# Seven groups of RWKV matmuls per head pair tied to fixed places in the projection's stream of set matmuls

## The chip, the cores and the metric

The kernel runs on one core of one Trainium2 chip. The metric is the device time of one launch, in microseconds. A core has a tensor engine (TensorE, PE in the profile), a vector engine (VectorE, DVE), a scalar engine (ScalarE, ACT), GpSimd (POOL) and a queue engine that starts transfers (SyncE, SP). Each engine works through its own list of instructions, whose order is settled when the kernel is built; between engines, semaphores hold an instruction back until what it needs is done.

## The reference

One block of a hybrid decoder, for 512 tokens of width 2048, all in float32. The projection `h @ w_in` feeds three things: an RWKV-7 mixer with 16 heads of 64, a sliding-window attention, and two sigmoid gates of 2048 columns each. The change concerns the mixer and the stretch in which it runs beside the projection.

```python
z = h @ w_in[l]
zs = token_shift(z[..., :RW_SHIFT_COLS], rw_mu[l])
o_rw = rwkv7_mix(zs, ...)            # 16 heads, 512 steps each
...
def step(state, inp):                # inside rwkv7_mix
    r_t, k_t, v_t, w_t, ka_t, kb_t = inp
    sa = einsum('bhvk,bhk->bhv', state, ka_t)
    state = state * w_t[:, :, None, :] + sa[..., None] * kb_t[:, :, None, :] + v_t[..., None] * k_t[:, :, None, :]
    y = einsum('bhvk,bhk->bhv', state, r_t)
    return state, y
...
y = group_norm(y) * gn_w + gn_b
out = (y + bonus) * g
...
x = x + (sigmoid(zg_rw) * (o_rw @ w_rw) + sigmoid(zg_att) * (o_att @ w_att)) @ w_out
x = x + conv_ffn(rms_norm(x, norm2_g[l]), w_up, conv_w, conv_b, w_down)
```

## The kernel before, in words

The program has three long parts: the projection with attention and the RWKV mixer beside it, the two output matrices, and the feed-forward network. All products of float32 are kept exact enough by splitting each operand into a high and a low part and adding three products (high by high, low by high, high by low).

**The stream of set matmuls.** `project` makes one projection tile of 128 columns by 512 tokens: 16 slices of the width, three matmuls each, 48 in all, into one PSUM tile `acc` (lines 263 to 265). Their weights come from `load_w`: a transfer into `raw` (L245), a copy to the high part `whi` on ScalarE (L248), a subtraction to the low part `wlo` on VectorE (L249); one load holds four slices, that is 12 set matmuls. I call these matmuls the stream, or set matmuls. They depend on nothing that the mixer does.

**The pairs.** The 16 heads are worked on two at a time, in eight pairs (0 to 7). The 512 tokens are cut into eight chunks of 64. For pair p, `late(p)` solves the recurrence; `early(p+1)` prepares the next pair, with its three projection tiles (k, r, v); `final(p)` normalises and gates the result; then three gate tiles are projected. So beside each pair run six tiles, 288 set matmuls. The steps of `late` and `final`, in order:

1. Masked products of each chunk (L634): 16 matmuls into four PSUM tiles from a rotation of three buffers named `bulk`; VectorE masks each (L638, L639).
2. The inverse of a triangular matrix per chunk. Its first level: transposes of BX (L651), VectorE and ScalarE work on them (L653, L655, splits at L212 and L213); transposes of BKK (L668) that ScalarE copies out (L669).
3. Transposes of `vz` (L672, the first group that the change names), which ScalarE copies to UV and SV (L678).
4. Five levels m = 2, 4, 8, 16, 32 that double the block solved: `mm3` with AI (L684, L685), the sum of two halves (ScalarE L697, VectorE L698), a mask (L708), a split into XIW (ScalarE L212, VectorE L213), then `mm3` with BT (the same lines; these are the second to sixth groups that the change names), its sum, and transposes of X (L730) whose copies give the next level's BT (L734).
5. A serial chain over the eight chunks: psG (L742), copied to GY (L743), psU (L745), copied to UV (L746 and L747), psS (L751), which updates the state SV (L755) for the next chunk.
6. Group norm of y on VectorE and ScalarE (L769 to L776), its last operation the product at L776.
7. `final`: transposes of y (L783, the seventh group), copied on ScalarE (L789), scaled and added on VectorE (L790, L791), six matmuls for the gate (L795), a product (L796) and a transfer out on POOL (L797).

**What sets the order.** The framework's scheduler lists every instruction and lays each engine's order out from the dependences and its own estimates of time, except where the code asks for program order. The mixer's groups are thereby strewn among set matmuls on TensorE, and the weight splits L248 and L249 among the mixer's work on ScalarE and VectorE. Whether a group waits on the chip depends on how many set matmuls stand ahead of it.

Of the kernel before, what the change touches and what calls it, by code (L numbers as in the profile page):

```python
# [18 lines left out]
P = 128  # L19
# [115 lines left out]
def block_kernel(ctx: ExitStack, tc: tile.TileContext, d: Dims, a: dict, out: bass.AP):  # L135
    nc = tc.nc
    act, dve, pool, pe, sync = nc.scalar, nc.vector, nc.gpsimd, nc.tensor, nc.sync
    NK, NP, NQ, NKV, NF = d.NK, d.NP, d.NQ, d.NKV, d.NF
# [19 lines left out]
    ident = const.tile([P, P], F32, name="ident")  # L158
# [61 lines left out]
    for f in range(NPRE):  # L220
        w, t = a["w_up"][f], {n: up_d[f, n] for n in ("s3", "s1", "P6", "P3")}
# [12 lines left out]
    def sums_along(jobs=jobs):  # L234
# [3 lines left out]
        pin(sync.dma_start(dst, first, max_dma_last_dim=4096))  # L238
        return lambda: pool.dma_start(dst, second, accum_op=ALU.add, max_dma_last_dim=4096)

    def load_w(src):
        nk, ncol = src.shape[1:]
        n = nk * ncol
        raw = wp["raw"].tile([P, 512], F32, name="raw", tag="raw")[:, :n].rearrange("p (k c) -> p k c", c=ncol)
        wp["last"] = sync.dma_start(raw, src)  # L245
        hi = wp["hl"].tile([P, 512], F32R, name="whi", tag="whi")[:, :n].rearrange("p (k c) -> p k c", c=ncol)
        lo = wp["hl"].tile([P, 512], F32R, name="wlo", tag="wlo")[:, :n].rearrange("p (k c) -> p k c", c=ncol)
        act.activation(hi, raw, AF.Copy)  # L248
        dve.tensor_tensor(lo, raw, hi.bitcast(F32), op=ALU.subtract)  # L249
        wp["n"] += 1  # L250
        if wp["n"] % wp["step"] == 0:
            sums_along()()
        return hi, lo

    def project(acc, src, xhi, xlo, pre=()):
        nk = src.shape[1]
        for k0 in range(0, nk, 4):
            n = min(4, nk - k0)
            whi, wlo = pre[k0 // 4] if k0 // 4 < len(pre) else load_w(src[:, k0 : k0 + n])
            for j in range(n):  # L260
                k = k0 + j
                first, last = k == 0, k == nk - 1
                pe.matmul(acc, whi[:, j], xhi[:, k], start=first, stop=False)  # L263
                pe.matmul(acc, whi[:, j], xlo[:, k], start=False, stop=False)  # L264
                pe.matmul(acc, wlo[:, j], xhi[:, k], start=False, stop=last)  # L265


    act.dma_start(par, a["par"])
# [17 lines left out]
    if True:  # L286
        xhi = by_k(big(big1, "xhi", "h1"))
        xlo = by_k(big(big1, "xlo", "l1"))
        zt = {c: a["w_z"][i].rearrange("p (k c) -> p k c", c=P) for i, c in enumerate(d.z_tiles())}
        with tc.tile_pool(name="x0_ps", bufs=6, space=PSUM) as ps0:  # L290
# [9 lines left out]
            first = {d.c_ka: [load_w(zt[d.c_ka][:, k0 : k0 + 4]) for k0 in range(0, min(NK, 12), 4)]}  # L300
# [22 lines left out]
        def emit_gate():  # L323
            if not gates:
                return
            i = gates.pop(0)
            acc = ztile(d.c_zr + i * P)
            g = gp.tile([P, S], F32, name="gt", tag="gt")
            act.activation(g, acc, AF.Tanh, scale=0.5)
            act.dma_start(gate_d[i * P : (i + 1) * P], g)  # L330
# [19 lines left out]
        with ExitStack() as pt:  # L350
# [32 lines left out]
            for t in range(NKV):  # L383
                acc = ztile(d.c_ka + t * P)
# [90 lines left out]
        with ExitStack() as pr:  # L475
# [131 lines left out]
            def late(p, st):  # L607
# [61 lines left out]
                    act.activation(W2[:, ns, 0:4:3], ps.rearrange("p n (h c) -> p n h c", c=C), AF.Copy)  # L669
                ps = bulk().rearrange("p (t c) -> p t c", c=P)  # L670
                for t in range(NT):
                    pe.transpose(ps[:, t], vz[:, t * P : (t + 1) * P], ident)  # L672
                for dst in (UV, SV):
                    dst = dst.rearrange("p (t w) h c -> p t w h c", w=2)
                    for w, (rl, rh) in enumerate(HV):
# [5 lines left out]

                def mm3(ps, wt, both, hi):
                    for n in range(NCH):
                        pe.matmul(ps[:, n], wt[:, 0, n], both(n), start=True, stop=False)  # L684
                        pe.matmul(ps[:, n, 0], wt[:, 1, n], hi(n), start=False, stop=True)  # L685

                def halves(m, t):
# [91 lines left out]
            def final(p, st):  # L779
                ag, bon, y = st  # L780
                ps = bulk().rearrange("p (t c) -> p t c", c=P)
                for t in range(NT):
                    pe.transpose(ps[:, t], y[:, t * P : (t + 1) * P], ident)  # L783
                yc = wtile("gn")
                dst = yc.rearrange("p (t w c) -> p t w c", w=2, c=C)
                for w, (rl, rh) in enumerate(HV):
                    for h, (lo, hi) in enumerate(HV):
                        ol, oh = HV[1 - h]
                        act.activation(dst[lo:hi, :, w], ps[rl:rh, :, ol:oh], AF.Copy)  # L789
                dve.tensor_scalar(yc, yc, col("gn_w", p), col("gn_b", p), op0=ALU.mult, op1=ALU.add)  # L790
                dve.tensor_tensor(yc, yc, bon, op=ALU.add)  # L791
                ps = bulk()
                for i in range(NG):
                    for j, (l, r) in enumerate(((0, 0), (0, 1), (1, 0))):
                        pe.matmul(ps, ag[l][:, i], gdz[r][:, i], start=i + j == 0, stop=i == NG - 1 and j == 2)  # L795
                dve.tensor_tensor(yc, yc, ps, op=ALU.mult)  # L796
                pool.dma_start(o_rw_d[p], yc)  # L797

            st = early(0)
            for p in range(NP):  # L800
                lt = late(p, st)
                if p + 1 < NP:
                    st = early(p + 1)
                final(p, lt)
                sums_along(up_jobs)()
                for _ in range(GATES_PER_PAIR * NK // 16):
                    emit_gate()


        xbs = ExitStack()  # L810
# [653 lines left out]
```

## Time and profile before

| what | value |
|---|---|
| median of three runs | 2811.76 us (2809.82 to 2811.87) |
| profiled execution, its own time | 2812.58 us |
| its span | 2810.7 us |
| TensorE busy | 2764.8 us (98%) |
| VectorE, ScalarE, POOL busy | 71%, 48%, 8% |
| start of pairs 0 to 7 (first L634) | 332.74, 431.79, 529.27, 626.90, 724.69, 822.33, 919.97, 1017.56 us |

The eight pairs fill the span from about 333 to 1115 us; all else lies outside the change. In a line of the profile's timeline stand start, duration, engine, line, operation, tiles, shapes, and in brackets how long the engine stood idle before and who released it. The two starts in the table for one pair may differ by 0.1 to 0.2 us from those of a row, where a row begins with a weight load.

### The profile page before, as it was taken

To read this page: it belongs to the slowest core of one execution; us is meant where nothing else is said; L and a number is where in the kernel's file an instruction comes from. 1 tells how busy PE (TensorE), PEld (TensorE's weight loads), DVE (VectorE), ACT (ScalarE), POOL (GpSimd) and SP (SyncE) were. 2 spreads that over 40 slices of the span, in tenths; PEclk is the share of its full clock that TensorE was granted. 3 is DMA by queue.
4 is the path that set the end of the run, shared out by engine and by line. 5 is a ranking of instruction groups with operands and counts; after the bars stand their busy time and mean duration, and the time that the engine had idled before them with its cause. 6 is when DMAs were issued, how large, how long until landed. Compare 5 with 4: busy or idle time off the path is not lost.

```text
span 2810.7 us, 45990 instructions
## 1 busy us (share of the span) xinstructions
PE 2764.8 (98%) x17466; PEld 2403.0 (85%) x17466; DVE 1990.5 (71%) x3452; ACT 1352.5 (48%) x2278; POOL 232.1 (8%) x307
## 2 busy tenths in 40 slices
PE   7999999999999999999999999999999999999999
PEld 5777777787777777888889999999999999888887
DVE  4588677777787775455678787777777778655555
ACT  4255445445544543322466555554555455444444
POOL 0001010110101001011000010101010101000000
PEclk9999999999999999999999999999999999999999
DMA  7855787777778777888785888988888888877775
GB/s 220 228 157 156 207 207 180 194 199 182 189 179 204 177 176 193 263 244 288 248 266 178 227 227 232 245 229 221 236 244 227 222 239 231 321 241 242 257 255 188
DMA packets 227182, 619.62 MB, mean 220 GB/s; under 512 B 24832, under 2 KB 44944, under 8 KB 225936
## 3 DMA queue, kind: packets, MB, share of 16 engines
q1 hardware_dynamic: 158400, 441.03, 48.5%
q0 software_dynamic: 37216, 136.33, 25.3%
q10 hardware_dynamic: 31344, 39.31, 4.0%
q8 instruction: 137, 2.24, 0.3%
q14 instruction: 85, 0.70, 0.1%
HBM read 566.96 MB, written 191.18 MB: 270 GB/s over the span
## 4 chain that ended last, share of the span: by engine, by line
PE 88%; DVE 6%; ACT 3%; issue 1%; DMA 1%; SPq 0%; ACTq 0%; DVEq 0%
PE X L1104 18%; PE X L968 11%; PE acc L264 9%; PE acc L263 9%; PE acc L265 9%; PE Y L1104 9%; PE Y L968 9%; PE Z L1104 4%; DVE wlo L249 1%; PE psS L751 1%; PE bulk L634 1%; PE psG L742 1%; PE bulk L684 1%; ACT whi L248 1%; PE mi L463 1%
## 5 line engine op out<-in xcount | busy, mean ns | idle before, releaser
L263 PE MATMUL acc<-xhi,whi 128*128 128x512 f32 x1152 | 463.4, 402 | 1.9 <-DVE xlo L309 1.9
L265 PE MATMUL acc<-xhi,wlo 128*128 128x512 f32 x1152 | 461.2, 400 | 0.0
L264 PE MATMUL acc<-xlo,whi 128*128 128x512 f32 x1152 | 460.6, 400 | 0.0
L248 ACT ACTIVATE whi<-raw 128x512 fp32r<-128x512 f32 x352 | 220.2, 630 | 376.0 <-PE acc L264 298.2
L961 DVE TENSOR_TENSOR wlo<-raw,whi 128x1024 fp32r<-128x1024 f32 x210 | 257.1, 1225 | 199.7 <-ACT whi L960 199.7
L249 DVE TENSOR_TENSOR wlo<-raw,whi 128x512 fp32r<-128x512 f32 x352 | 241.7, 689 | 169.4 <-ACT whi L248 155.0
L960 ACT ACTIVATE whi<-raw 128x1024 fp32r<-128x1024 f32 x210 | 222.7, 1061 | 283.8 <-PE X L968 137.0
L1087 DVE TENSOR_TENSOR wlo<-raw,whi 128x1024 fp32r<-128x1024 f32 x184 | 224.8, 1223 | 77.5 <-ACT whi L1085 77.2
L1104 PE MATMUL X<-b,whi 128*128 128x256 f32 x1472 | 268.9, 283 | 0.2 <-ACT whi L1085 0.2
L1104 PE MATMUL X<-t,whi 128*128 128x256 f32 x1408 | 257.2, 283 | 1.4 <-ACT u L1132 1.4
L1104 PE MATMUL Y<-t,whi 128*128 128x256 f32 x1408 | 257.1, 283 | 0.0
L263 PEld LDWEIGHTS acc<-xhi,whi 128*128 128x128 f32 x1152 | 217.5, 189 | 41.5 <-DVE xlo L309 2.1
L264 PEld LDWEIGHTS acc<-xlo,whi 128*128 128x128 f32 x1152 | 217.6, 189 | 39.8 <-issue 1.7
L265 PEld LDWEIGHTS acc<-xhi,wlo 128*128 128x128 f32 x1152 | 217.3, 189 | 39.8 <-issue 0.9
L1104 PEld LDWEIGHTS X<-b,whi 128*128 128x128 f32 x1472 | 229.6, 192 | 0.5 <-ACT whi L1085 0.4
L1085 ACT ACTIVATE whi<-a 128x1024 fp32r<-128x1024 f32 x124 | 130.9, 1056 | 201.6 <-DVE a L1080 193.7
L1104 PEld LDWEIGHTS X<-t,whi 128*128 128x128 f32 x1408 | 219.6, 192 | 1.6 <-ACT u L1132 1.6
L1104 PEld LDWEIGHTS Y<-t,whi 128*128 128x128 f32 x1408 | 219.6, 192 | 0.0
L1104 PE MATMUL X<-b,wlo 128*128 128x256 f32 x736 | 208.5, 283 | 0.9 <-DVE wlo L1087 0.9
L1085 ACT ACTIVATE whi<-raw 128x1024 fp32r<-128x1024 f32 x184 | 192.9, 1049 | 22.8 <-ACT whi L1085 14.1
L1087 DVE TENSOR_TENSOR wlo<-a,whi 128x1024 fp32r<-128x1024 f32 x124 | 152.0, 1226 | 67.5 <-ACT whi L1085 66.9
L1104 PE MATMUL X<-t,wlo 128*128 128x256 f32 x704 | 199.5, 283 | 0.2 <-DVE wlo L1087 0.2
(387 smaller groups left out, 5801.7 us busy)
## 6 DMA issues: line engine op xcount, KB each, us to landing
raw<-in_w_up_dram SPq DMA_DIRECT2D x170, 512.0 KB
raw<-in_w_z_dram SPq DMA_DIRECT2D x288, 256.0 KB
s_dn<-in_w_dn_dram POOLq DMA_DIRECT2D x88, 512.0 KB, 6.6
raw<-s_dn SPq DMA_DIRECT2D x88, 512.0 KB
raw<-in_w_up_dram POOLq DMA_DIRECT2D x80, 512.0 KB, 8.5
raw<-in_w_dn_dram SPq DMA_DIRECT2D x66, 512.0 KB
s_dn<-in_w_dn_dram SPq DMA_DIRECT2D x44, 512.0 KB
s_dn<-s_dn SPq DMA_DIRECT2D x44, 512.0 KB
```

What stands on the lines that cost most here:

```text
L248: act.activation(hi, raw, AF.Copy)
L249: dve.tensor_tensor(lo, raw, hi.bitcast(F32), op=ALU.subtract)
L263: pe.matmul(acc, whi[:, j], xhi[:, k], start=first, stop=False)
L264: pe.matmul(acc, whi[:, j], xlo[:, k], start=False, stop=False)
L265: pe.matmul(acc, wlo[:, j], xhi[:, k], start=False, stop=last)
L463: pe.matmul(ps, vhl[:, n - 1 + kb, g].rearrange("p e c -> p (e c)"), phl[i][:, kb].rearrange("p h c -> p (h c)"), start=kb == kbs[0] and i ...
L960: act.activation(whi, wr, AF.Copy)
L961: dve.tensor_tensor(wlo, wr, whi.bitcast(F32), op=ALU.subtract)
L968: pe.matmul(dst, l[:, q, ts], r[:, es], start=fst and j == 0, stop=lst and j == 2, skip_group_check=True)
L1085: pin(act.activation(hi, t, AF.Copy))
L1087: return lambda: pin(dve.tensor_tensor(lo, t, hi.bitcast(F32), op=ALU.subtract))
L1104: pin(pe.matmul(ps, l[:, k], r[:, k], start=start and k + i == 0, stop=last and i == 2, skip_group_check=True))
```

## The change

A list `stream` takes every set matmul in program order. Of each pair a list `entries` takes seven instructions: the first transpose of vz, the first BT matmul of each of the five levels, and the first transpose of y. For pairs 1 to 6, each entry gets an ordering dependence (no semaphore, only a rule for the scheduler) behind the set matmul that is the 23rd, 46th, 75th, 102nd, 127th, 154th or 282nd since the pair began. Pairs 0 and 7 get none.

```diff
+    stream = []
+
+    def behind(ins, before):
+        tc.add_manual_dep(ins.ins, before.ins.name,
+                          mybir.DependencyInfo(mybir.DependencyClass.NoSync, mybir.DependencyReason.DATA))
+
...
-                pe.matmul(acc, whi[:, j], xhi[:, k], start=first, stop=False)
-                pe.matmul(acc, whi[:, j], xlo[:, k], start=False, stop=False)
-                pe.matmul(acc, wlo[:, j], xhi[:, k], start=False, stop=last)
+                stream.append(pe.matmul(acc, whi[:, j], xhi[:, k], start=first, stop=False))
+                stream.append(pe.matmul(acc, whi[:, j], xlo[:, k], start=False, stop=False))
+                stream.append(pe.matmul(acc, wlo[:, j], xhi[:, k], start=False, stop=last))
...
-                    pe.transpose(ps[:, t], vz[:, t * P : (t + 1) * P], ident)
+                    ins = pe.transpose(ps[:, t], vz[:, t * P : (t + 1) * P], ident)
+                    if t == 0:
+                        entries.append(ins)
...
-                        pe.matmul(ps[:, n], wt[:, 0, n], both(n), start=True, stop=False)
+                        ins = pe.matmul(ps[:, n], wt[:, 0, n], both(n), start=True, stop=False)
+                        if wt is BT and n == 0:
+                            entries.append(ins)
...
-                    pe.transpose(ps[:, t], y[:, t * P : (t + 1) * P], ident)
+                    ins = pe.transpose(ps[:, t], y[:, t * P : (t + 1) * P], ident)
+                    if t == 0:
+                        entries.append(ins)
...
+            entries = []
+            ZT = 3 * NK
+            LATER = (23, 46, ZT + 27, 2 * ZT + 6, 2 * ZT + 31, 3 * ZT + 10, 5 * ZT + 42)
             st = early(0)
             for p in range(NP):
+                entries.clear()
+                base = len(stream)
                 lt = late(p, st)
...
+                if 0 < p < NP - 1:
+                    for ins, at in zip(entries, LATER):
+                        behind(ins, stream[base + at - 1])
```

ZT is 48, the set matmuls of a tile. Every engine executes the same instructions as before; only their order differs, from pair 1 on. In set matmuls since the pair's first L634, pairs 2 to 6 (pair 1 in brackets where it differs):

| group | before | after |
|---|---|---|
| vz transposes | 21 | 23 |
| BT of level 2 | 46 | 47 (46) |
| BT of level 4 | 73 | 75 |
| BT of level 8 | 98 | 102 |
| BT of level 16 | 121 | 127 |
| BT of level 32 | 146 | 154 |
| first psG, last psS | 146, 230 | 154, 238 |
| y transposes | 264 | 282 |
| next pair's L634 | 288 | 288 |

In the new code the lines stand 6 to 12 further down: the set matmuls at 269 to 271, the splits at 254 (ScalarE) and 255 (VectorE), L634 as 640, L638 and L639 as 644 and 645, `mm3` as 692 and 695, L783 as 793, L795 as 807, L796 as 808.

On TensorE, at the end of pair 2, around the transposes of y (the numbers tell one buffer from the next; `whi_6480` is a weight load, after which `whi_6500` and `whi_6518` are the last two that the pair's stream uses):

```order
L264 MATMUL acc_6459<-xlo_203,whi_6480 128x512
L265 MATMUL acc_6459<-xhi_202,wlo_6481 128x512
L783 MATMUL bulk_6278<-ident_162,yc_5836 128x128 x4
L795 MATMUL bulk_6290<-gdhi_2606,wghi_4875 128x512
L795 MATMUL bulk_6290<-gdlo_2607,wghi_4875 128x512
L795 MATMUL bulk_6290<-gdhi_2606,wglo_4876 128x512
```

Before, y stood at the end of load 6480's twelve set matmuls, with the 24 of the two last loads still behind it. After the change:

```order
L270 MATMUL acc_6459<-xlo_203,whi_6518 128x512
L271 MATMUL acc_6459<-xhi_202,wlo_6519 128x512
L793 MATMUL bulk_6278<-ident_162,yc_5836 128x128 x4
L807 MATMUL bulk_6290<-gdhi_2606,wghi_4875 128x512
L807 MATMUL bulk_6290<-gdlo_2607,wghi_4875 128x512
L807 MATMUL bulk_6290<-gdhi_2606,wglo_4876 128x512
```

Now y stands in the middle of the last load, 6518: eighteen set matmuls moved from behind y to ahead of it, and six are left between the gate's matmuls and the next pair's L634.

Also on TensorE, at level 4 of pair 2 (XIW by BT into a `bulk` tile); the weights with the number 6144 and 6145 are one load, whose first set matmul stood directly ahead of the group:

```order
L264 MATMUL acc_6105<-xlo_203,whi_6126 128x512
L265 MATMUL acc_6105<-xhi_202,wlo_6127 128x512
L263 MATMUL acc_6105<-xhi_202,whi_6144 128x512
L684 LDWEIGHTS BT_2939
L684 MATMUL bulk_5632<-XIW_5457,BT_2939 128x64
L685 LDWEIGHTS BT_2939
```

After the change:

```order
L270 MATMUL acc_6105<-xlo_203,whi_6126 128x512
L271 MATMUL acc_6105<-xhi_202,wlo_6127 128x512
L269 MATMUL acc_6105<-xhi_202,whi_6144 128x512
L270 MATMUL acc_6105<-xlo_203,whi_6144 128x512
L271 MATMUL acc_6105<-xhi_202,wlo_6145 128x512
L692 LDWEIGHTS BT_2939
L692 MATMUL bulk_5632<-XIW_5457,BT_2939 128x64
```

The group now has the two further set matmuls L270 and L271 ahead of it.

On VectorE, at the boundary from pair 2 to pair 3, from the split after y's last product to the first masks of the next pair:

```order
L249 TENSOR_TENSOR wlo_7085<-raw_7082,whi_7084 128x512
L790 TENSOR_SCALAR gn_6283<-gn_6283,par_164 128x512
L213 TENSOR_TENSOR wglo_7056<-wl_7053,wghi_7055 128x256
L791 TENSOR_TENSOR gn_6283<-gn_6283,bon_5186 128x512
L796 TENSOR_TENSOR gn_6283<-gn_6283,bulk_6290 128x512
L249 TENSOR_TENSOR wlo_7103<-raw_7100,whi_7102 128x512
L249 TENSOR_TENSOR wlo_7121<-raw_7118,whi_7120 128x512
L638 TENSOR_TENSOR AB_2940<-bulk_6549,cst_168 128x256
L639 TENSOR_TENSOR W2_2937<-bulk_6549,cst_168 128x2x128
L638 TENSOR_TENSOR AB_2940<-bulk_6554,cst_168 128x256
L639 TENSOR_TENSOR W2_2937<-bulk_6554,cst_168 128x2x128
L646 TENSOR_TENSOR tt_6548<-AB_2940,cst_168 64x256
```

After the change:

```order
L786 TENSOR_TENSOR yc_5836<-yc_5836,rg1_5947 128x512
L255 TENSOR_TENSOR wlo_7103<-raw_7100,whi_7102 128x512
L802 TENSOR_SCALAR gn_6283<-gn_6283,par_164 128x512
L213 TENSOR_TENSOR wglo_7056<-wl_7053,wghi_7055 128x256
L803 TENSOR_TENSOR gn_6283<-gn_6283,bon_5186 128x512
L808 TENSOR_TENSOR gn_6283<-gn_6283,bulk_6290 128x512
L255 TENSOR_TENSOR wlo_7121<-raw_7118,whi_7120 128x512
L644 TENSOR_TENSOR AB_2940<-bulk_6549,cst_168 128x256
L645 TENSOR_TENSOR W2_2937<-bulk_6549,cst_168 128x2x128
L644 TENSOR_TENSOR AB_2940<-bulk_6554,cst_168 128x256
L645 TENSOR_TENSOR W2_2937<-bulk_6554,cst_168 128x2x128
L644 TENSOR_TENSOR AB_2940<-bulk_6559,cst_168 128x256
```

Of the two weight splits that stood between the gate's product and the first mask (L638, now L644) one is left, and the product L646 has gone from among the masks to behind them.

## The prediction

> **What bounds the kernel now.** I read the page first: busy time of each engine, the chain that ended last, the costliest groups.
>
> ```profile
> PE 2764.8 (98%) x17466; PEld 2403.0 (85%) x17466; DVE 1990.5 (71%) x3452; ACT 1352.5 (48%) x2278; POOL 232.1 (8%) x307
> ...
> PE 88%; DVE 6%; ACT 3%; issue 1%; DMA 1%; SPq 0%; ACTq 0%; DVEq 0%
> ...
> L263 PE MATMUL acc<-xhi,whi 128*128 128x512 f32 x1152 | 463.4, 402 | 1.9 <-DVE xlo L309 1.9
> ...
> L248 ACT ACTIVATE whi<-raw 128x512 fp32r<-128x512 f32 x352 | 220.2, 630 | 376.0 <-PE acc L264 298.2
> ...
> L249 DVE TENSOR_TENSOR wlo<-raw,whi 128x512 fp32r<-128x512 f32 x352 | 241.7, 689 | 169.4 <-ACT whi L248 155.0
> ```
>
> TensorE is the bound, so a new order can win only what TensorE stands still, and the set matmuls of this line hardly wait themselves (1.9 us in 1152). The two splits of their weights, 0.63 us on ScalarE and 0.69 on VectorE, serve below. The table by stage shows the pairs that the change touches; each stretch runs from one pair's first L634 to the next.
>
> ```profile
> core 0: us, PE busy (x) PEld busy (x) DVE busy (x) ACT busy (x) POOL busy (x), PEclk, DMA share, GB/s
> ...
> 431.79:529.27 97.48, 96.06 (x636) 77.06 (x635) 75.25 (x182) 47.78 (x107) 9.87 (x13) 1.00 0.75 190
> 529.27:626.90 97.63, 96.22 (x637) 77.21 (x635) 75.37 (x182) 47.93 (x107) 9.85 (x13) 1.00 0.75 189
> ```
>
> A pair lasts 97.63 us at full clock with 1.4 us of idle TensorE; no engine beside it is near its limit. The waits of six pairs name whom TensorE waits for:
>
> ```profile
> PE bulk L684 <- DVE XIW L213: 4.3, 12, 0.6
> PE bulk L783 <- DVE yc L776: 2.7, 6, 0.5
> ```
>
> That is two waits a pair at L684 and one at L783, two of the kinds of groups that the change ties down. The busy end of a matmul is modelled, so I price each wait by starts instead. Here is the timeline of TensorE in pair 2: the set matmul ahead of each of the seven groups, and the group's first instruction; and one group (L751) that didn't wait.
>
> ```profile
> 539.11 0.47 PE L265 MATMUL acc<-xhi,wlo 128*128 128x512 f32 x1
> 539.60 0.66 PE L672 MATMUL bulk<-ident,vz 128*128 128x128 f32 x4
> ...
> 546.34 0.39 PE L263 MATMUL acc<-xhi,whi 128*128 128x512 f32 x1
> 547.27 0.20 PE L684 MATMUL bulk<-XIW,BT 128*128 128x64 f16 x1 [0.54 <-DVE XIW L213]
> ...
> 554.80 0.39 PE L263 MATMUL acc<-xhi,whi 128*128 128x512 f32 x1
> 555.35 0.20 PE L684 MATMUL bulk<-XIW,BT 128*128 128x64 f16 x1 [0.16 <-DVE XIW L213]
> ...
> 562.36 0.39 PE L264 MATMUL acc<-xlo,whi 128*128 128x512 f32 x1
> 562.86 0.20 PE L684 MATMUL bulk<-XIW,BT 128*128 128x64 f16 x1
> ...
> 569.39 0.39 PE L263 MATMUL acc<-xhi,whi 128*128 128x512 f32 x1
> 569.72 0.20 PE L684 MATMUL bulk<-XIW,BT 128*128 128x64 f16 x1
> ...
> 576.73 0.39 PE L264 MATMUL acc<-xlo,whi 128*128 128x512 f32 x1
> 577.23 0.20 PE L684 MATMUL bulk<-XIW,BT 128*128 128x64 f16 x1
> ...
> 610.35 0.40 PE L264 MATMUL acc<-xlo,whi 128*128 128x512 f32 x1
> 610.67 0.66 PE L751 MATMUL psS<-UV,W 128*128 128x64 f32 x4
> 611.14 0.48 PE L265 MATMUL acc<-xhi,wlo 128*128 128x512 f32 x1
> ...
> 618.73 0.39 PE L265 MATMUL acc<-xhi,wlo 128*128 128x512 f32 x1
> 619.57 0.66 PE L783 MATMUL bulk<-ident,yc 128*128 128x128 f32 x4 [0.45 <-DVE yc L776]
> ...
> 621.46 0.39 PE L263 MATMUL acc<-xhi,whi 128*128 128x512 f32 x1
> ...
> 626.90 3.61 PE L634 MATMUL bulk<-BAR,BKK 128*128 128x256 f32 x16
> ```
>
> Between the last two rows lie 24 set matmuls in 5.44 us: one each 0.227 us. The gaps less 0.23 are the waits: 0.70 us at level 2 (BT2), then 0.32, 0.27, 0.10 and 0.27 at levels 4, 8, 16 and 32, and 0.61 at y. For the vz transposes, 0.49 less the 0.32 of the unwaiting L751 leaves 0.17. Together 2.44 us a pair.
>
> **The change, part by part.** No instruction is added or removed; only orders change, from pair 1 on. Positions below are counts of set matmuls since the pair's first L634, read in the two orders.
>
> *Levels 4 to 32, pairs 1 to 6.* Their BT groups go from positions 73, 98, 121 and 146 to 75, 102, 127 and 154, so each gets two more set matmuls than before after the group ahead of it, 0.45 us of cover. Every wait priced there (0.10 to 0.32) is shorter, so all four go, 0.96 us a pair. If the small transfers ahead of them came later by as much, nothing would be won: bounds 0 and 0.96. I take 0.96, as cover exceeds each wait.
>
> *y, pairs 1 to 6.* The last L751 moves from position 230 to 238 and y from 264 to 282, so 44 set matmuls instead of 34 stand between. The rows give 0.47 us for L751's group (610.67 to 611.14) and 44 x 0.227 = 9.99: TensorE reaches y 10.46 us after L751, where y was ready at 8.90 (619.57 less 610.67). The 0.61 us goes. Sum so far 1.57 us a pair.
>
> *vz and BT2, all pairs.* The vz transposes move from 21 to 23 and their 0.17 us goes or shrinks, but BT2 is reached from them by a chain that already makes TensorE wait 0.70, so what vz saves BT2 waits. Priced at nothing.
>
> *The boundary: what y's new place costs.* Y's tail must pass ScalarE and VectorE before the next pair's first masks (L638). Rows of the boundary from pair 2 to 3, on ScalarE and VectorE:
>
> ```profile
> 620.26 1.55 ACT L789 ACTIVATE gn<-bulk 64x256 f32<-64x256 f32 x4 [0.70 <-PE bulk L783]
> ...
> 621.85 0.66 DVE L790 TENSOR_SCALAR gn<-gn,par 128x512 f32<-128x512 f32 x1 [1.56 <-ACT gn L789]
> ...
> 623.47 0.69 DVE L796 TENSOR_TENSOR gn<-gn,bulk 128x512 f32<-128x512 f32 x1
> ...
> 627.53 0.69 DVE L249 TENSOR_TENSOR wlo<-raw,whi 128x512 fp32r<-128x512 f32 x1 [2.02 <-ACT whi L248]
> ...
> 628.14 0.42 DVE L638 TENSOR_TENSOR AB<-bulk,cst 128x256 f32<-128x256 f32 x1
> ```
>
> Before, L634 came 7.33 us after y (626.90 less 619.57), and its first mask 1.24 us later. Now six set matmuls are left between: L783 and L795 take 1.89 (619.57 to 621.46), six matmuls 1.36, so L634 comes 3.25 us after y. L796 ends 4.59 us after y (624.16), which is 1.34 after L634; one weight split (0.61 from its start to L638's) stands between, so the first mask starts about 1.95 instead of 1.24, some 0.7 us late. The fourth L634 tile waits for a PSUM buffer that the first tile's L639 frees (three buffers, four tiles), and the chain L638, L645, L651, L655, L669, L678, L697, L708, L213 to BT2 follows. Laying that chain out in the new order with these durations, BT2 starts 18.79 us after L634 instead of 18.00 (547.27 less 529.27, the start of pair 2): 0.79 us later. Pairs 2 to 6 now have one more set matmul ahead of BT2 (47 for 46), so the net loss is 0.79 less 0.23, 0.56 each; pair 7, whose own positions stay, loses 0.79. Bounds for one head: nothing, if the chain has room that I don't see, and 1.6, twice my figure, if two more VectorE operations of 0.4 us come ahead. I take 0.79, the layout from rows.
>
> VectorE's row at 628.14 stands right behind the split's 0.61 us, and TensorE's 547.27 behind 0.54 us of idle although hundreds of set matmuls were queued: neither engine passes what stands ahead. [...]
>
> *Serial chain psG, psU, psS.* It moves 6 to 8 set matmuls later as a block; a weight split now precedes one of ScalarE's copies there. I charge 0.09 us a pair; bounds 0 and 0.3.
>
> *POOL and SP.* POOL's clearing of BAR now stands behind one accumulating DMA issue, and one weight load stands ahead of the row-sum DMAs on SP:
>
> ```profile
> 607.98 1.10 POOL L765 MEMSET BAR<- 64x512 f32 x2 [9.73 <-PE psG L742]
> 609.88 0.81 POOL L239 DMA_DIRECT2D s_dn<-in_w_dn_dram  x1 [0.81 <-DMA s_dn<-in_w_dn_dram]
> ```
>
> That DMA issue ends at 610.69, the clearing then at 611.79, 15 us ahead of the L634 that needs it. Nothing; without that cover it would be the 2.7 us by which it moved.
>
> **The sum.** Pair 1: 1.57 won. Pairs 2 to 6: 1.57 less 0.56, 1.01 each, 5.05. Pair 7: 0.79 lost. Serial chain: 6 x 0.09 = 0.54 lost. Won in all 1.57 + 5.05 - 0.79 - 0.54 = 5.3 us. The profiled execution took 2812.58 us, 0.8 above the median 2811.76, and would become 2807.3; against the median 2806.5. No more than 6 x 2.44 = 14.6 can be won by taking waits away.
>
> **The rivals.** *The boundary is free.* If L638 isn't later, pairs 2 to 6 win 1.57 + 0.23, and pair 7 loses nothing: 6 x 1.57 + 5 x 0.23 - 0.54 = 10.0 us, 2801.8. For it: VectorE idles 1.56 us ahead of L790 in the rows, and the order of masks is a little tighter. Against: the split and L796 stand ahead of L638, one queue.
>
> *The head costs double.* At 1.6 us a boundary six heads lose 4.9 us more: 0.4 won, 2811.3. For it: three buffers for four tiles, so any lateness of L796 (it frees one of them) delays L634 itself; against: L796 would have to miss its time by 0.8.
>
> *Slower: the tail collides.* The place is VectorE between L796 and L638. If L790 waits for one split more on ScalarE, and L638 for one more on VectorE whose weights TensorE hasn't released yet (0.63 and 0.69, plus that release), a head costs 2.6 us. It decides from 0.79 + 5.3/6 = 1.67 a boundary; at 2.6 the total is 5.6 slower, 2817.4. For it: six set matmuls are few, and before L249 waited 2 us for a split of ScalarE ahead of L638. Against: the order puts only one split there, not two.
>
> **How the numbers follow.** A difference of 0.2%, 5.6 us, is about what a measurement of this kernel tells from none. My forecast, 3 to 8 us won: 0.52, half of it beyond 5.6. Free boundary: 0.20. Double head cost: 0.14. Collision: 0.14. Faster 0.26 + 0.20 = 0.46, same 0.26 + 0.14 = 0.40, slower 0.14. The range leaves out the collision alone: 2801.5, just past the free boundary, to 2812.5, just past the double head cost.
>
> **What the profile after would show.** Right: no idle ahead of y and of the BT groups of levels 4 to 32 in pairs 1 to 6; pair 1's stretch near 96.0 us, 2 to 6 near 96.7, pair 7's head 0.8 longer; BT2 waiting some 0.1 more. Wrong: L638 over 2 us after L634, an idle ahead of L634's third or fourth tile beyond 0.3 us, L651 or psU waiting, or a set matmul waiting for its weights.

## The result

The changed kernel takes 2802.64 us (median of 8 runs, 2801.53 to 2805.01) against 2810.90 us for the kernel before on the same chip (8 runs, 2809.00 to 2812.22). The ratio is 0.9972 with a 95% interval of 0.9961 to 0.9982: faster by 5.1 to 11.0 us, where 5.3 us were forecast. The time lies inside the stated range, 2801.5 to 2812.5.

The profiled execution after took 2802.24 us, with a span of 2800.5. The table by stage, each stretch from one pair's first L640 (the old L634) to the next, for pairs 1, 2, 3 and 6:

```profile
core 0: us, PE busy (x) PEld busy (x) DVE busy (x) ACT busy (x) POOL busy (x), PEclk, DMA share, GB/s
426.82:522.97 96.15, 95.52 (x637) 77.53 (x635) 74.14 (x181) 47.91 (x107) 9.15 (x12) 1.00 0.77 192
522.97:619.68 96.71, 95.91 (x636) 77.28 (x635) 75.13 (x183) 48.03 (x107) 9.80 (x13) 1.00 0.77 190
619.68:716.38 96.70, 95.95 (x636) 77.28 (x635) 75.23 (x183) 48.06 (x107) 9.73 (x13) 1.00 0.78 192
909.81:1006.61 96.80, 95.99 (x636) 77.29 (x635) 75.20 (x182) 47.62 (x106) 9.74 (x13) 1.00 0.75 188
```

Pair 1 takes 96.15 us and a pair of 2 to 6 some 96.7, where 97.6 stood before and 96.0 and 96.7 had been forecast. From the start of pair 1 to the end of the span the two traces differ by 5.4 us (2810.7 - 431.6 = 2379.1 before, 2800.5 - 426.8 = 2373.7 after); from pair 1's start to pair 7's start it is 6.0. The other 4.8 us of the difference between these two executions lie ahead of pair 1, where the order of every engine is the same; the experiments come back to that.

The waits of TensorE in pairs 1 to 6 after the change, in the view of waits:

```profile
PE bulk L692 <- DVE XIW L213: 3.9, 6, 0.7
```

Of twelve waits for XIW six are left, one a pair, and the six for y are gone. The timeline of TensorE in pair 2 shows which are left: the set matmul ahead of each BT group (levels 2, 4, 8, 16, 32), of y and of the next pair's products.

```profile
540.48 0.39 PE L270 MATMUL acc<-xlo,whi 128*128 128x512 f32 x1
541.56 0.20 PE L692 MATMUL bulk<-XIW,BT 128*128 128x64 f16 x1 [0.69 <-DVE XIW L213]
...
549.51 0.39 PE L271 MATMUL acc<-xhi,wlo 128*128 128x512 f32 x1
549.74 0.20 PE L692 MATMUL bulk<-XIW,BT 128*128 128x64 f16 x1
...
557.20 0.39 PE L271 MATMUL acc<-xhi,wlo 128*128 128x512 f32 x1
557.43 0.20 PE L692 MATMUL bulk<-XIW,BT 128*128 128x64 f16 x1
...
564.41 0.39 PE L269 MATMUL acc<-xhi,whi 128*128 128x512 f32 x1
564.64 0.20 PE L692 MATMUL bulk<-XIW,BT 128*128 128x64 f16 x1
...
572.10 0.39 PE L269 MATMUL acc<-xhi,whi 128*128 128x512 f32 x1
572.33 0.20 PE L692 MATMUL bulk<-XIW,BT 128*128 128x64 f16 x1
...
616.26 0.39 PE L271 MATMUL acc<-xhi,wlo 128*128 128x512 f32 x1
616.49 0.38 PE L793 MATMUL bulk<-ident,yc 128*128 128x128 f32 x2
...
619.45 0.39 PE L271 MATMUL acc<-xhi,wlo 128*128 128x512 f32 x1
619.68 0.38 PE L640 MATMUL bulk<-BAR,BKK 128*128 128x256 f32 x1
```

Levels 4 to 32 and y now follow their set matmul at 0.23 us, the pace of the stream: no wait. Level 2 follows at 1.08, a wait of 0.85 instead of 0.70, and comes 18.59 us after the pair's first L640 (541.56 less 522.97) instead of 18.00. The boundary from pair 2 to 3 on VectorE, much like the one ahead of pair 2, shows how that begins:

```profile
620.22 0.69 DVE L808 TENSOR_TENSOR gn<-gn,bulk 128x512 f32<-128x512 f32 x1
620.83 0.69 DVE L255 TENSOR_TENSOR wlo<-raw,whi 128x512 fp32r<-128x512 f32 x1
621.43 0.42 DVE L644 TENSOR_TENSOR AB<-bulk,cst 128x256 f32<-128x256 f32 x1
```

The gate's product ends at 620.91, 1.23 us after the next pair's first L640 (619.68), one weight split follows, and the first mask starts 1.75 us after that L640, where it was 1.24.

### The profile page after: what moved, and what is told of

It is laid out like the page before. It is cut to its first block, busy times and chain, and to the rows that moved or that the text cites. A ratio compares the mean times of both kernels' runs of the same rounds, so it can differ in the third digit from the quotient of the medians.

```text
span 2800.5 us, 45992 instructions
## 1 busy us (share of the span) xinstructions
PE 2759.3 (99%) x17466; PEld 2400.8 (86%) x17466; DVE 1988.9 (71%) x3452; ACT 1352.9 (48%) x2278; POOL 231.3 (8%) x307
## 4 chain that ended last, share of the span: by engine, by line
PE 63%; DVE 2%; DMA 1%; ACT 1%; issue 0%; ACTq 0%; DVEq 0%; SPq 0%
PE X L1124 17%; PE X L988 10%; PE Y L988 9%; PE Y L1124 9%; PE acc L270 4%; PE acc L269 4%; PE acc L271 4%; PE Z L1124 4%; DMA raw<-in_w_dn_dram 1%; DVE wlo L1107 0%; DVE c L1176 0%; PE psS L761 0%; ACT whi L1105 0%; PE ps_t L1054 0%; PE psG L752 0%
## 5 line engine op out<-in xcount | busy, mean ns | idle before, releaser
L270 PE MATMUL acc<-xlo,whi 128*128 128x512 f32 x1152 | 459.8, 399 | 0.0
L271 PE MATMUL acc<-xhi,wlo 128*128 128x512 f32 x1152 | 459.5, 399 | 0.0
L271 PEld LDWEIGHTS acc<-xhi,wlo 128*128 128x128 f32 x1152 | 216.8, 188 | 40.0 <-issue 0.9
L270 PEld LDWEIGHTS acc<-xlo,whi 128*128 128x128 f32 x1152 | 217.0, 188 | 39.4 <-issue 1.7
```

The costliest lines, as they stand in the source:

```text
L270: stream.append(pe.matmul(acc, whi[:, j], xlo[:, k], start=False, stop=False))
L271: stream.append(pe.matmul(acc, wlo[:, j], xhi[:, k], start=False, stop=last))
```

## The experiments

Each kernel differs from the changed one in its ties alone. The table gives the mean stretch of pairs 2 to 6, the time from pair 1's start to pair 7's start, both from one trace each, and the ratio of the runs to those of the kernel before on the same chip. The traces repeat a stretch within some 0.1 us (only one stretch, pair 6 of e12 with 95.82, stands further out), so they tell apart what the runs, with intervals of about 5 us in all, do not.

| kernel | pairs 2 to 6, us each | pair 1 to pair 7, us | median, us | ratio, 95% interval |
|---|---|---|---|---|
| before | 97.63 | 585.8 | 2810.1 to 2810.9 | |
| changed | 96.73 | 579.8 | 2802.64 | 0.9972 (0.9961 to 0.9982) |
| e1 no ties | 97.63 | 585.8 | 2811.10 | 1.0003 (0.9994 to 1.0012) |
| e2 vz and levels, y free (275) | 96.64 | 579.8 | 2804.23 | 0.9975 (0.9966 to 0.9984) |
| e3 y alone, 282 | 97.57 | 584.8 | 2809.83 | 1.0001 (0.9992 to 1.0010) |
| e4 level 2 at 50 | 96.60 | 579.1 | 2805.49 | 0.9980 (0.9971 to 0.9989) |
| e5 y alone, 267 | 96.97 | 581.9 | 2806.36 | 0.9983 (0.9974 to 0.9992) |
| e6 as changed, y at 278 | 96.11 | 576.7 | 2801.49 | 0.9966 (0.9953 to 0.9978) |
| e7 trimmed | 96.01 | 576.1 | 2799.01 | 0.9958 (0.9946 to 0.9971) |
| e8 ties to level 4 | 97.14 | 582.8 | 2807.80 | 0.9990 (0.9981 to 0.9999) |
| e9 even cover | 95.35 | 572.0 | 2796.27 | 0.9952 (0.9938 to 0.9966) |
| e10 even cover, y at 278 | 95.35 | 572.1 | 2795.57 | 0.9953 (0.9941 to 0.9966) |
| e11 and pair 7 | 95.35 | 572.1 | 2794.66 | 0.9945 (0.9932 to 0.9957) |
| e12 and pair 0 | 95.44 | 572.5 | 2795.63 | 0.9948 (0.9936 to 0.9961) |

The theory was that of the prediction: TensorE's waits at single groups are what can be won; cover wins each of them at levels 4 to 32 and at y, and y's late place gives part of it back at the next pair's head. The rivals were that y, or the levels, carries it alone; that the pair is bound by the mixer's own chain, so that a wait removed comes back at the next group; and that part of the gain came with the new program and not with its order.

### e1: the list of set matmuls, without ties

```diff
-            LATER = (23, 46, ZT + 27, 2 * ZT + 6, 2 * ZT + 31, 3 * ZT + 10, 5 * ZT + 42)
+            LATER = ()
```

> The list of set matmuls is kept and no group is tied, so every engine has the order of before. If the whole gain comes from the waits of pairs 1 to 7: 2810.9 us within 1.5, pairs 2 to 6 at 97.6 us each. If the part of the gain that lies ahead of pair 1 (3.9 us up to pair 0's start and 0.9 in pair 0, where the order is the same) came with the new program and not by chance: about 2808, with pair 0 starting near 329 us. If that part is a matter of the granted clock in single executions, pair 0 starts near 329 where the clock is 1.00 all the way, and up to 4 us later where a slice shows less.

The time is that of before, 1.0003 (0.9994 to 1.0012), and the pairs take 97.63 us, so no gain comes with the program itself. Pair 0 starts at 330.34 us, between the two other traces (332.74 before, 328.86 after). The granted clock tells them apart in part. Here are two stretches ahead of pair 1, of the kernel before:

```profile
30.00:40.00 10.00, 8.09 (x31) 5.58 (x32) 5.82 (x14) 4.08 (x11) 0.81 (x1) 0.83 0.40 80
325.00:335.00 10.00, 7.29 (x29) 5.72 (x28) 9.74 (x16) 3.54 (x7) 1.63 (x2) 0.90 0.97 225
```

Of the kernel without ties:

```profile
30.00:40.00 10.00, 8.09 (x41) 6.30 (x40) 6.11 (x15) 4.54 (x12) 0.82 (x1) 1.00 0.40 80
325.00:335.00 10.00, 7.32 (x26) 5.67 (x25) 9.93 (x19) 2.35 (x6) 0.81 (x1) 0.83 0.94 190
```

And of the changed kernel:

```profile
30.00:40.00 10.00, 8.09 (x41) 5.89 (x40) 5.99 (x14) 4.31 (x11) 0.82 (x1) 1.00 0.41 81
325.00:335.00 10.00, 7.96 (x35) 6.16 (x34) 9.86 (x21) 2.65 (x6) 0.81 (x1) 1.00 0.97 226
```

The column before the last two is the granted clock. The profiled execution of before had a dip in both places, the one without ties in the second, the changed one in neither. In the same stretch the same list of instructions then gets through 31 or 41 matmuls. The first dip follows waits of TensorE at the start (the last 1.9 us, for VectorE's xlo, in the traces of before and of changed alike), the second a wait at pair 0's first masked products (2.7 us at L634 before, 2.7 at L640 without ties), and whether one comes differs between kernels whose order there is the same. The two dips make up about half of the 4.8 us ahead of pair 1. After the first, TensorE starts its 100th matmul at 44.3 us where the changed kernel has 42.8, and with the second pair 0 takes 98.89 us against 97.97. The rest is TensorE's waiting ahead of pair 0: for VectorE's BAR 2.7 us before and 1.5 after, and for ScalarE's phi 1.0 us before and none after. The clock doesn't settle when pair 0 starts: in all fourteen traces TensorE, VectorE, ScalarE and POOL work through the same order up to there, and pair 0 starts anywhere from 328.5 to 332.7 us; e7, which has the first dip (0.84 from 30 to 45 us), starts it at 328.56. So the 4.8 us are a matter of these two executions and not of the change. That such chance also explains why the medians of eight runs differ by 8.3 us and the traces from pair 1 on by 5.4 is likely but not shown, since only one run of each kernel has a trace.

### e2 and e3: the two halves of the change

```diff
-            LATER = (23, 46, ZT + 27, 2 * ZT + 6, 2 * ZT + 31, 3 * ZT + 10, 5 * ZT + 42)
+            LATER = (23, 46, 75, 102, 127, 154)
```

> The tie of y is left out; the vz and level ties stay, and y comes at 275 instead of 282. If the levels' cover carries the gain and y at 282 costs the next pair's head 0.37 us net: the head is as before (BT of level 2 at 18.0 us after L634 instead of 18.6), y waits 0 to 0.2, pairs 2 to 6 at 96.1 to 96.4 us, total 2800 to 2801.5. If y needs the seven further set matmuls: it waits 0.5 to 0.6 again, pairs at 96.7 to 96.9 and total 2802.5 to 2804.

For y alone, a zero leaves a group free:

```diff
-            LATER = (23, 46, ZT + 27, 2 * ZT + 6, 2 * ZT + 31, 3 * ZT + 10, 5 * ZT + 42)
+            LATER = (0, 0, 0, 0, 0, 0, 282)
...
                     for ins, at in zip(entries, LATER):
-                        behind(ins, stream[base + at - 1])
+                        if at:
+                            behind(ins, stream[base + at - 1])
```

> Only y is tied (282); the levels keep the scheduler's places. If the levels carry the gain: y wins 0.61 a pair and the head gives back 0.37 and 0.2, pairs 2 to 6 at 97.5 to 97.7 us, total 2810 to 2811. If y carries it: pairs near 97.0 and total 2807.

With the levels alone the pairs take 96.64 us and the way from pair 1 to pair 7 579.8, the same as with y tied. Pairs 2 to 6 are 0.25 to 0.5 us above what I expected, because y waits more than the 0 to 0.2 that I gave it. On TensorE, pair 3 of this kernel:

```profile
712.65 0.39 PE L270 MATMUL acc<-xlo,whi 128*128 128x512 f32 x1
713.31 0.33 PE L793 MATMUL bulk<-ident,yc 128*128 128x128 f32 x1 [0.28 <-DVE yc L786]
```

0.66 less 0.23 is a wait of 0.43 at y; level 2 is back at 18.0 us after the pair's start. With y alone at 282 the pairs take 97.57, a win of 0.06 us each: the 0.61 at y goes and the head takes it back, level 2 coming at 18.65 and its transposes waiting. So the levels carry the change, and tying y at 282 was worth nothing in pairs 2 to 6. It moved a wait from one pair's tail to the next pair's head; only pair 1, whose head has no tied pair ahead of it, wins by y alone (96.99 us for 97.64).

### e4: cover for level 2 as well

```diff
-            LATER = (23, 46, ZT + 27, 2 * ZT + 6, 2 * ZT + 31, 3 * ZT + 10, 5 * ZT + 42)
+            LATER = (23, 50, 78, 105, 130, 157, 282)
```

> Level 2 is tied at 50 instead of 46, the levels after it three later than in the changed kernel (78, 105, 130, 157), y at 282 as there. If the level-2 wait of 0.85 us is a plain lack of set matmuls ahead: it falls to 0.1, and pairs 2 to 6 take 95.9 to 96.1 us, total 2798 to 2799. If the chain behind it only gets as much later: the wait shows up at the next group, pairs at 96.7, total 2802.6.

The pairs take 96.60 us, where 95.9 to 96.1 was expected of plain cover. Level 2 and y in pair 3, on TensorE:

```profile
639.81 0.39 PE L270 MATMUL acc<-xlo,whi 128*128 128x512 f32 x1
640.20 0.20 PE L692 MATMUL bulk<-XIW,BT 128*128 128x64 f16 x1
...
714.26 0.39 PE L271 MATMUL acc<-xhi,wlo 128*128 128x512 f32 x1
714.88 0.33 PE L793 MATMUL bulk<-ident,yc 128*128 128x128 f32 x1 [0.23 <-DVE yc L786]
```

Level 2's wait fell from 0.85 to 0.16, but y, with the same place in the stream, waits 0.39 again, and two groups of transposes some 0.1 each. The levels had been pushed later by three and the last psS by seven, to 245. So 37 set matmuls are left between it and y, as many as in e2 (275 less 238), where y waits about as long. The pairs' 96.60 us lie near the 96.7 of the rival, a pair bound by the mixer's chain.

### e5 and e6: where y costs nothing

```diff
-            LATER = (23, 46, ZT + 27, 2 * ZT + 6, 2 * ZT + 31, 3 * ZT + 10, 5 * ZT + 42)
+            LATER = (0, 0, 0, 0, 0, 0, 267)
...
                     for ins, at in zip(entries, LATER):
-                        behind(ins, stream[base + at - 1])
+                        if at:
+                            behind(ins, stream[base + at - 1])
```

> Only y is tied, at 267 instead of the scheduler's 264 (and not at 282). If y at 282 was worth nothing by itself only because it came so late that the next pair's head paid: three set matmuls cover the 0.61 us, the head stays (BT of level 2 at 18.0 us after L634), pairs 2 to 6 take 97.0 to 97.1 us, total 2807. If the next pair's head pays for any later y, because the chain from y to L638 bounds the pair: 97.5 to 97.6, total 2810.

```diff
-            LATER = (23, 46, ZT + 27, 2 * ZT + 6, 2 * ZT + 31, 3 * ZT + 10, 5 * ZT + 42)
+            LATER = (23, 46, 75, 102, 127, 154, 278)
```

> The ties of the changed kernel, with y at 278 between the 275 of the levels-only kernel and 282. If both ends lose a little (0.43 us of wait for y at 275, 0.6 us later masks at 282): y no longer waits, the gate's product ends 0.4 us after the next L634 and one weight split fits before the first mask, the head stays at 18.0 and pairs 2 to 6 take 95.9 to 96.2 us, total 2798 to 2799.5. If the head pays for each place gained: 96.6, total 2802.

Three set matmuls more ahead of y, and nothing else, bring the pairs from 97.63 to 96.97, the whole 0.61 us; the head stays at 17.98. With the levels tied and y at 278 they take 96.11. The stage of pair 3 of that kernel, then y, and VectorE at the next boundary:

```profile
620.66:716.75 96.09, 95.45 (x636) 77.50 (x635) 75.35 (x183) 47.95 (x107) 9.76 (x13) 1.00 0.76 192
```

```profile
712.43 0.39 PE L270 MATMUL acc<-xlo,whi 128*128 128x512 f32 x1
712.66 0.38 PE L793 MATMUL bulk<-ident,yc 128*128 128x128 f32 x2
...
716.75 0.59 PE L640 MATMUL bulk<-BAR,BKK 128*128 128x256 f32 x2
```

```profile
716.40 0.69 DVE L808 TENSOR_TENSOR gn<-gn,bulk 128x512 f32<-128x512 f32 x1
717.39 0.69 DVE L255 TENSOR_TENSOR wlo<-raw,whi 128x512 fp32r<-128x512 f32 x1 [0.30 <-ACT whi L254]
718.00 0.42 DVE L644 TENSOR_TENSOR AB<-bulk,cst 128x256 f32<-128x256 f32 x1
```

y doesn't wait, the gate's product ends 0.34 us after the next L640 (717.09 less 716.75), and the first mask comes 1.25 us after it, as in the kernel before. Both ends fit. The stretches came as expected; the total was to be 2798 to 2799.5 and is 2801.49, so my translation of stretches into a total was 2 us off, within what the runs scatter.

### e7: cover taken from the levels that have too much

By then the traces told when each level's input was ready. In the changed kernel XIW was ready 0.19 us ahead of its matmul at level 4, but 1.35, 0.86 and 0.60 ahead at levels 8, 16 and 32 (the end of VectorE's L213 against the start of L692).

```diff
-            LATER = (23, 46, ZT + 27, 2 * ZT + 6, 2 * ZT + 31, 3 * ZT + 10, 5 * ZT + 42)
+            LATER = (23, 50, 79, 102, 125, 150, 276)
```

> Ties at 23, 50, 79, 102, 125, 150 and 276: level 2 gets the cover that it lacks, levels 8, 16 and 32 give up the 0.6 to 1.3 us by which their input was ready early. If the pair is bound by TensorE's work plus the waits of single groups: hardly a wait is left, pairs 2 to 6 take 95.4 to 95.8 us, total 2795 to 2798. If the mixer's chain from L634 to y bounds the pair, as the wait that came back at y with level 2 at 50 suggests: more than 96.3, total above 2800.

96.01 us a pair lies between the two expectations. Level 2 waits no more and level 4's input is now 1.34 early; levels 8 to 32 (which the scheduler put at 103, 127 and 151) wait 0.13 each and y 0.21. Cover is not the whole of it: a weight split has come to stand directly ahead of VectorE's L213, so that the way from one level's first BT matmul to the XIW of the next takes 7.08 us at levels 8, 16 and 32, where the changed kernel has 6.34, 6.34 and 7.08. With 24 set matmuls for that way each of them just misses. That pointed to cover in the wrong places rather than to a bound by the chain; e9 and e10 test it.

### e8: what removed level 8's wait

```diff
-            LATER = (23, 46, ZT + 27, 2 * ZT + 6, 2 * ZT + 31, 3 * ZT + 10, 5 * ZT + 42)
+            LATER = (23, 46, 75)
```

> Only vz, level 2 and level 4 are tied (23, 46, 75); the scheduler then puts level 8 at 96, 21 set matmuls after level 4 (25 before, 27 in the changed kernel). If the number of set matmuls ahead is what removed level 8's wait: level 8 waits 1.1 us or more, and pairs 2 to 6 take 97.3 to 98 us. If it was the shorter chain of the small transfers, which have no weight split among them now (level 4 to level 8 in 6.35 us instead of 7.48): level 8 waits 0.1 to 0.3, and pairs take 96.6 to 97.2.

Level 8 stands at 96, with 21 set matmuls after level 4 instead of the 25 of before. TensorE in pair 3:

```profile
654.90 0.39 PE L271 MATMUL acc<-xhi,wlo 128*128 128x512 f32 x1
655.21 0.20 PE L692 MATMUL bulk<-XIW,BT 128*128 128x64 f16 x1
```

With four set matmuls fewer it waits 0.08 us, less than the 0.27 of before. So the count of matmuls ahead doesn't decide that wait alone. VectorE between the second half of level 4 and level 8's XIW, in pair 2 before:

```profile
559.51 0.42 DVE L734 COPY BT<-bulk 64x512 f16<-64x512 f16 x1 [1.46 <-ACT BT L734]
559.96 0.43 DVE L698 TENSOR_TENSOR tt<-bulk,tt 128x256 f32<-128x256 f32 x1
560.30 0.68 DVE L249 TENSOR_TENSOR wlo<-raw,whi 128x512 fp32r<-128x512 f32 x1
561.01 0.43 DVE L734 COPY BT<-bulk 64x512 f16<-64x512 f16 x1
561.47 0.42 DVE L708 TENSOR_TENSOR tt<-tt,cst 128x256 f32<-128x256 f32 x1
562.38 0.43 DVE L213 TENSOR_TENSOR XIW<-tt,XIW 128x256 f16<-128x256 f32 x1 [0.48 <-ACT XIW L212]
```

And in the changed kernel:

```profile
552.98 0.69 DVE L255 TENSOR_TENSOR wlo<-raw,whi 128x512 fp32r<-128x512 f32 x1 [0.54 <-ACT whi L254]
553.84 0.42 DVE L744 COPY BT<-bulk 64x512 f16<-64x512 f16 x1 [0.17 <-ACT BT L744]
554.29 0.42 DVE L708 TENSOR_TENSOR tt<-bulk,tt 128x256 f32<-128x256 f32 x1
554.75 0.43 DVE L718 TENSOR_TENSOR tt<-tt,cst 128x256 f32<-128x256 f32 x1
555.20 0.43 DVE L744 COPY BT<-bulk 64x512 f16<-64x512 f16 x1
555.66 0.42 DVE L213 TENSOR_TENSOR XIW<-tt,XIW 128x256 f16<-128x256 f32 x1
```

Before, a weight split and a copy stood between the sum (L698) and its mask (L708): 1.51 us from one to the other. Now the mask (L718) follows the sum (L708) at 0.46, and the split went ahead of both, where VectorE had been idle. The way from level 4's first BT matmul to the XIW of level 8 shrank from 7.46 us (555.35 to the end at 562.81) to 6.34 (549.74 to 556.08). The kernel of e8 has the same order there, the mask 0.46 behind the sum and the same 6.34 us:

```profile
653.35 0.42 DVE L708 TENSOR_TENSOR tt<-bulk,tt 128x256 f32<-128x256 f32 x1
653.81 0.42 DVE L718 TENSOR_TENSOR tt<-tt,cst 128x256 f32<-128x256 f32 x1
```

The ties changed not only TensorE's list: the scheduler laid the weight splits elsewhere among VectorE's small steps too. In the changed kernel either would have covered level 8's 0.27 us, the two further set matmuls (0.45 us) or the shorter way (1.1 us).

### e9 to e12: even cover, and the end pairs

```diff
-            LATER = (23, 46, ZT + 27, 2 * ZT + 6, 2 * ZT + 31, 3 * ZT + 10, 5 * ZT + 42)
+            LATER = (23, 50, 76, 101, 126, 151, 277)
```

> Ties at 23, 50, 76, 101, 126, 151 and 277: 26 set matmuls to level 4 instead of 29, which was 1.3 us more than it needed, 25 to each level after it, and y one later than in the trimmed kernel. If waits of single groups are all that is left to win: the waits of 0.13 at levels 8 to 32 and 0.21 at y go, and pairs 2 to 6 take 95.3 to 95.6 us, total 2796 to 2797.5. If the chain from L634 to y now bounds the pair: 95.9 to 96.1 as in the trimmed kernel, total 2799.

```diff
-            LATER = (23, 46, ZT + 27, 2 * ZT + 6, 2 * ZT + 31, 3 * ZT + 10, 5 * ZT + 42)
+            LATER = (23, 50, 77, 102, 127, 152, 278)
```

> As the run with even cover, but level 4 with 27 set matmuls ahead and all after it one later (77, 102, 127, 152, 278). If one matmul of cover is what level 4 or y lacks there: 95.2 to 95.5 us a pair, total 2796 to 2797. If nothing lacked: within 0.1 us of the other a pair.

Both bring the pairs to 95.35 us, from the end of the expectation that single waits are all that is left. The stages of pairs 2 and 3 of the second:

```profile
522.15:617.50 95.35, 95.26 (x637) 77.51 (x636) 75.29 (x183) 47.95 (x107) 9.77 (x13) 1.00 0.77 194
617.50:712.82 95.32, 95.23 (x637) 77.51 (x636) 75.41 (x183) 47.96 (x107) 9.74 (x13) 1.00 0.78 194
```

TensorE is busy but for 0.1 us a pair, and its view of waits from pair 1 to pair 7 is empty. In e9 the way to levels 8, 16 and 32 is 6.34 us each, so two things differ from e7: one set matmul more, and no weight split on the way. But level 32 of e10 doesn't wait with 7.08 us and 25 set matmuls, so 25 were enough with either. The rival of a chain-bound pair falls: the chain fits into TensorE's work if the cover is laid where it is needed. That e9 and e10 take the same time says no single matmul of cover lacked. The e10 ties were then given to pair 7, behind the gate tiles that follow it, and to pair 0:

```diff
                 if 0 < p < NP - 1:
                     for ins, at in zip(entries, LATER):
                         behind(ins, stream[base + at - 1])
+                if p == NP - 1:
+                    tail = list(zip(entries, [base + at - 1 for at in LATER]))
...
             while gates:
                 emit_gate()
+            for ins, at in tail:
+                if at < len(stream):
+                    behind(ins, stream[at])
```

> The same ties also for pair 7, behind the gate tiles that follow it. If pair 7's waits (0.7 at level 2, 0.2, 0.3, 0.1, 0.2 at the others and 0.4 at y) go as in the other pairs: 1.5 to 2 us less than without, total 2794.5 to 2796. If what follows pair 7 waits for its result: no change, or its later y costs up to 2 us.

For pair 0, beside that:

```diff
-                if 0 < p < NP - 1:
+                if p < NP - 1:
```

> The same ties for pairs 0 and 7 too. If pair 0 loses its waits as the others did: pair 0 takes 95.5 to 97 us instead of 98.0, total 1 to 2 us less than with pair 7 alone. If the start of the stage bounds it: 98.

In pair 7 all waits go but one of 0.45 us at y, which comes 87.94 us after the pair's start with 278 set matmuls done, where e10 has 269 done at 87.16: nine more, 2.0 us of work, for 0.78 us, a win of 1.3. The medians, 2795.57 without and 2794.66 with it, don't tell this apart. Pair 0 takes 97.59 us in an execution with a dip of the clock at its start, 1.3 less than in the three other traces with such a dip (98.89 to 98.98). Level 2 still waits 0.5 us there and vz 0.3, since the ties at 50 and 23 ask for no more than the 50 and 25 that the scheduler gave them. The total shows no gain. The kernel with pair 7 has the lowest median, 0.9945 of the kernel before (0.9932 to 0.9957), twice the win of the change studied here.

## Why the prediction was right, and where it was not

*The bound and the price of the waits* held. TensorE's stretch lost what the gaps between starts had shown: the four level waits and y's went to the pace of the stream in all six tied pairs of the changed kernel.

*The sum held by its parts.* Pair 1 won 1.49 us (1.57 less 0.09 forecast), pairs 2 to 6 0.90 on the mean (0.92 by the forecast's terms). That the parts fit so closely is in part luck, as the next three paragraphs show. At y too the way was longer than I took it: its input came 9.36 us after the last psS instead of 8.84, and was still 1.2 us early.

*The head was the right price with a different make-up.* The first mask came 1.75 us after L640 (forecast 1.95, before 1.24) and level 2 at 18.59 (forecast 18.79, before 18.00). The gate's product, the split and the mask stand one behind the other on VectorE and start 0.61 and 0.60 us apart (620.22, 620.83, 621.43). The net loss there is 0.37 us and not 0.56. What I had not in the sum is the wait of the level-2 transposes (L740), 0.26 us instead of 0.05 in pairs 2 to 6, which nearly makes up the difference.

*Pair 7 was mis-sized.* Forecast to lose 0.79, it has level 2 at 18.25 instead of 17.97, a loss of 0.28. I gave it the whole layout of the new order, but its own list is that of before. In pair 2 level 2 comes 0.35 later than that, and the rows show where it arises: the first mask starts 0.1 later (1.73 us after L640 against 1.62), the BX transposes 0.16 (6.43 against 6.27), and ScalarE's first copy to UV the whole 0.35 (12.50 against 12.15). ScalarE makes a copy to W (L675) first in pair 7, and in pair 2 only behind a split into XIW (L212). Pairs 2 to 6 have the BX transposes at 12 and 21 instead of 11 and 20, but that place isn't what delays them: they wait for their input there, 0.1 us, and in pair 7 0.28. A wait at L651 (now L657) was among my signs of being wrong; it came, and is small.

*"All four go, as cover exceeds each wait" was right in what happened and incomplete in why.* I had the bounds right (0 and 0.96) and took the cover as the reason. At levels 8, 16 and 32 the chain of small steps got shorter as well: the way from the level before to XIW went from 7.46 us to 6.34, from 6.80 to 6.34 and from 7.46 to 7.08. By these figures either the cover or the shorter chain would have removed each wait; only for level 8 does a run show the one without the other (e8). Level 4 in pairs 2 to 6 is luck. It has 28 set matmuls after level 2 where it had 27, one more and not the two that I counted, 0.23 us against a wait of 0.32. Its wait went because the level-2 transposes between them wait 0.2 us longer, the same 0.2 that I had not in the sum. The prediction read VectorE's order at the boundary, but not between the levels.

*The three rivals.* A free boundary, worth 10.0 us in the forecast, is not what the change has, but it is what y at 278 makes of it (e6): there a pair wins 1.52 us, the 1.57 less 0.09 of the forecast, without the 0.23 of a further set matmul ahead of level 2. The double head cost and the collision did not come: the tail keeps a head's cost at half a microsecond because only one split stands ahead of the first mask.

*The total* moved by 8.3 us where the parts that changed order account for 5.4 in the traces. The interval of the runs begins at 5.1, so they don't contradict each other. From pair 7's start to the end the fourteen traces scatter from 1792.0 to 1796.0 us, so a trace's total is no closer than that either.

## What to carry to other kernels

Where one engine is full and its waits sit at known groups, read for each group how early its input is ready, and spread the independent work by that: 25 or so matmuls of cover at each level, with y at 277 or 278, won 2.3 us a pair; the ties of the change won 1.5 with y at 278 and 0.9 with y at 282. A tie at the end of a stage is paid or won at the head of the next one, so try its place from both sides; y lost 0.43 us at 275, cost the head 0.6 at 282 and neither at 278. A tie on one engine's list can move other engines' lists as well, and a step off the chain that stands in it (the weight split here) may be worth more than the cover, as at level 8, 1.1 us against 0.45: read the orders of the other engines between the tied groups too.

## What was not expected of the hardware

The granted clock dips at two places ahead of pair 1 in some executions. In the traces of before and of e1 a dip shows as 0.83 to 0.90 over ten microseconds. In the first dip of before the stream's matmuls follow each other at 0.43 us (36.47 to 39.45 us) instead of 0.23. From 30 to 45 us eight of the fourteen traces show 0.84 or 0.89 and the six others 1.00. At the start of pair 0 a dip came in four of the fourteen, behind waits of TensorE of 1.9 to 2.7 us, while a wait of 2.2 us in another trace (e9) brought none. In the order of before, pair 0 takes 98.9 to 99.0 us with such a dip, and 97.9 to 98.1 without one. What brings a dip about these traces don't show. Differences of this size between two single traces say nothing of a change that begins later.
